# Head results of a two-layer hybrid encoder: adding two partial products ahead of the transposes, two heads to a set of four

## The chip, the cores and the metric

The kernel runs on one core of one Trainium2 chip. The metric is the device time of one execution in microseconds (us). The core has a matrix engine (PE, with its weight loads shown as PEld), a vector engine (DVE), a scalar engine (ACT), GpSimd (POOL), and a queue (SP) that issues transfers.

## The reference

A trunk of two layers over 512 positions of width 1024. Each layer is a half-step SwiGLU block, a token mixing, and another half-step SwiGLU block; each is normalised, shifted, scaled and gated by a conditioning vector. The change lies in the token mixing alone:

```python
oa, _ = banded_attention(qa, ka, va, A_HALF_WINDOW, sink)      # 8 query heads, 2 key heads
for window, dilation in B_BRANCHES:                            # 8 heads, three branches
    o, l = dilated_branch(qb, kb, vb, window, dilation)
...
ya = rmsnorm(oa.reshape(b, s, A_WIDTH), onorm_a)
yb = rmsnorm(ob.reshape(b, s, B_WIDTH), onorm_b)
return jnp.concatenate([ya, yb], axis=-1) @ w_out
```

Every head has dimension 64. Of the 16 heads of a layer, the eight "b" heads attend to all 512 keys under a mask and the eight "a" heads to a window of 128 on either side. Everything is float32.

## The kernel before

Products keep float32 accuracy by splitting an operand into a high and a low part (names ending in `h`/`hi` and `l`/`lo`) and adding several products. In the mixing, a layer's 16 heads run one after the other, the eight b heads (0 to 7) first and the eight a heads (8 to 15) next. Two consecutive heads, with `a` = 0 and 1, share one projected query tile.

A head's work (`class Head`) has four steps. `scores(qt)`, for each of four blocks of 128 queries, makes two score products (L655, L656), adds the mask and takes the row extreme on DVE (L660), and takes the exponential on ACT with the row sum into a column of `den` (L664). `exps` adds the sink term for a heads (L671, L672) and inverts `den` (L673). `pv(kt)`, for each of four blocks of keys, transposes the exponentials on PE (L685), splits them on ACT and DVE (L688, L689), and accumulates two products into the PSUM tile `po` (L692, L693). The stationary operand there is `V2[kt][:, vh]`, whose 128 columns are the 64 of the high part of the values and the 64 of the low part. So `po` is 128 partitions by 512 queries: partitions 0 to 63 hold the result of the high part and 64 to 127 that of the low part. `finish` copies `po` to SBUF as `oT` (L697, ACT), transposes it in four blocks of 128 queries (L700, PE, into the PSUM tile that the code calls `p2` and the trace `p`), copies the 64 columns of the low part into the output `o` or `oa` (L702, ACT), adds the 64 columns of the high part (L703, DVE), and multiplies by the inverted sums (L704, DVE).

The tile `oT` has the tag `acc` with one buffer, which the accumulator of the next norm uses as well. The PSUM tiles `po` and `p2` come out of the pool `pm` with the tag `mm`, four banks that the projections and the output products also use.

The order on the engines is settled when the program is built: a planner with costs of its own takes the instructions by priority as their inputs come due, and each engine then runs its list in order. `heads_` gives the order in which the steps are written: while head n does `pv`, head n+1 does `scores`, then `finish` of head n follows.

```python
for j in range(4):
    cur.pv(j)
    ...
    if nxt:
        nxt.scores(j)
...
with tc.high_priority(offset=HF if (n, 4) in after else 0):
    cur.finish()
```

`weave` puts fill work between these steps: the projections of queries, keys and values (L215 to L217, L624 to L626) beside the b heads, and the half of the output product that needs the b heads alone (`fill_a`) from head 10 on. After head 7 `branch_norm(o)` normalises the b results (L767 to L777); `branch_t` transposes them (L783) at four places of heads 9 and 10. After head 15 the same happens to the a results, and `out_tiles` makes the other half of the output product. The weight splits (L146, L147), the residual (L366), the rotary embedding (L575 to L581) and the split of the values (L633, L634) share ACT, DVE and POOL with the heads.

Of the kernel before, what the change touches and what calls it, by code (L numbers as in the profile page):

```python
# [10 lines left out]
F32 = mybir.dt.float32  # L11
F32R = mybir.dt.float32r
I32 = mybir.dt.int32
AF = mybir.ActivationFunctionType
ALU = mybir.AluOpType
# [4 lines left out]
S = 512  # L20
# [39 lines left out]
def tile_trunk(ctx: ExitStack, tc: tile.TileContext, xT, c, positions, adaT, cols, sink, wi1, wo1,  # L60
               wqk, wv, w_out, wi2, wo2, masks, freqs, out):
    nc = tc.nc
    V, A, T, G = nc.vector, nc.scalar, nc.tensor, nc.gpsimd
# [4 lines left out]
    nrm = ctx.enter_context(tc.tile_pool(name="nrm", bufs=2))  # L68
    tiny = ctx.enter_context(tc.tile_pool(name="tiny", bufs=4))
# [492 lines left out]
    def mixer(l, norm, pool, mod):  # L562
# [47 lines left out]
        def vproj():  # L610
            for _ in range(4):
                V2.append(pool.tile([128, 10, 2, 64], F32R, tag=f"v{len(V2)}", name="v2"))
            for a in range(2):
# [21 lines left out]
                                        op=ALU.subtract)  # L635
                vdone.append(a)

        class Head:
            def __init__(self, q, a, k, ka, vh, o, oc, windowed, sc):
                self.q, self.a, self.k, self.ka, self.vh = q, a, k, ka, vh  # L640
                self.o, self.oc, self.sc = o, oc, sc
                self.win = windowed
                self.rng = [(max(qt - 1, 0), min(qt + 2, 4)) if windowed else (0, 4) for qt in range(4)]
                self.sm = []

            def scores(self, qt):
                if qt == 0:
                    self.nb = tiny.tile([128, 4], F32, tag="nb", name="nb")
                    self.den = tiny.tile([128, 4], F32, tag="den", name="den")
                k0, k1 = self.rng[qt]  # L650
                w = (k1 - k0) * 128
                ks = slice(k0 * 128, k1 * 128)
                p = pq.tile([128, S], F32, tag="s", name="s")
                lq = self.q[:, self.a, qt * 128:qt * 128 + 128]
                T.matmul(p[:, :w], lq, self.k[0][:, self.ka, ks], start=True, stop=False)  # L655
                T.matmul(p[:, :w], lq, self.k[1][:, self.ka, ks], start=False, stop=True)  # L656
                s = pool.tile([128, S], F32, tag="sm", name="sm", bufs=5)
                m0 = 896 + (128 if qt == 0 else 0) if self.win else 384 - 128 * qt
                least = 3.0e38 if self.sc is None else nsnk[:, self.sc:self.sc + 1]
                V.tensor_tensor_reduce(out=s[:, :w], in0=p[:, :w], in1=mask[:, m0:m0 + w], scale=-0.125,  # L660
                                       scalar=least, op0=ALU.add, op1=ALU.min,
                                       accum_out=self.nb[:, qt:qt + 1])
                self.sm.append(s)
                A.activation(s[:, :w], s[:, :w], AF.Exp, scale=-1.0, bias=self.nb[:, qt:qt + 1],  # L664
                             accum_out=self.den[:, qt:qt + 1])
# [27 lines left out]
                T.matmul(po, lv, pl[:, :w], start=False, stop=kt == 3, skip_group_check=self.win)  # L693

            def finish(self):
                oT = nrm.tile([128, S], F32, tag="acc", name="oT", bufs=1)
                A.activation(oT, self.po, AF.Copy)  # L697
                p2 = pm.tile([128, 4, 128], F32, tag="mm", name="p2")
                for qt in range(4):
                    T.transpose(p2[:, qt], oT[:, qt * 128:qt * 128 + 128], ident)  # L700
                od = self.o()[:, :, self.oc * 64:self.oc * 64 + 64]
                A.activation(od, p2[:, :, 64:128], AF.Copy)  # L702
                V.tensor_tensor(od, p2[:, :, 0:64], od, op=ALU.add)  # L703
                V.tensor_tensor(od, od, self.den[:, :, None].to_broadcast([128, 4, 64]), op=ALU.mult)  # L704

        def heads(makers, hp, after):
            it = heads_(makers, after)
# [295 lines left out]
    for l in range(L):  # L1003
        if l:
            with tc.tile_pool(name="ffn", **FP) as pool:
                ada["pool"] = pool, 1
                ada_list += [(1, ch, k) for ch in range(6, 9) for k in range(KD)]
                norm = ffn(l, 0, norm, pool, ada_step, mod=(fin[:, l, 4], fin[:, l, 3]))
                while ada_list:
                    ada_step()  # L1010
        with tc.tile_pool(name="mix", **FP) as pool:
            norm = mixer(l, norm, pool, (fin[:, l, 7], fin[:, l, 6]))
        with tc.tile_pool(name="ffn", **FP) as pool:
            ada["pool"] = pool, 1
            if l == 0:
                ada_list += [(1, ch, k) for ch in range(2, 6) for k in range(KD)]

            def gain(m, s):
                xg = pool.tile([128, 1024], F32, tag=f"s{'hl'[m % 2]}{m // 2}", name="xg")[:, :S] if s.start == 0 else xgs[m]
                if s.start == 0:  # L1020
                    xgs.append(xg)
                A.activation(xg[:, s], x[:, m, s], AF.Copy, scale=col[:, C_FIN + m:C_FIN + m + 1])

            xgs = []
            norm = ffn(l, 2, norm, pool, ada_step, None, gain if l == L - 1 else None,
                       (fin[:, 1, 1], fin[:, 1, 0]))
            while ada_list:
                ada_step()
            if l == L - 1:
                final_out(norm, xgs, pool)  # L1030
# [83 lines left out]
```

## Time and profile before

| | |
|---|---|
| median of 3 runs | 1953.99 us (1951.84 to 1955.06) |
| the profiled execution, its time | 1955.42 us |
| its span, first to last instruction | 1953.6 us |
| mean granted clock of PE, share of full speed | 0.993 |

The span is what the trace covers; 1.8 us of the profiled execution's time lie around it. An engine's busy time is the sum of its instructions' durations with overlaps taken once. Matrix products are pipelined, so the cost of one in a busy stretch is the distance from its start to the next one's start, not its duration.

### The profile page before, as it was taken

How to read it: one execution, taken by the hardware profiler on the slowest of the kernel's cores; microseconds unless marked ns; L12 is line 12 of the kernel's file. 1: busy time of each engine (PE TensorE's matmuls, PEld its weight loads, DVE VectorE, ACT ScalarE, POOL GpSimd, SP SyncE). 2: the span in 40 equal slices, each digit the busy share in tenths (PEclk: the TensorE clock that was granted, in tenths of full speed). 3: DMA queues.
4: the chain of work that ended last, by engine and by line, in shares of the span. 5: the costliest groups of instructions: out<-in, count | busy, mean ns of one | idle time of the engine just before them, and what ended most of it. 6: DMA issues, size and time to landing. Idle time of an engine off the chain costs nothing.

```text
span 1953.6 us, 31187 instructions
## 1 busy us (share of the span) xinstructions
PE 1915.1 (98%) x12064; PEld 1718.1 (88%) x12064; DVE 1510.1 (77%) x2713; ACT 939.2 (48%) x1798; POOL 94.9 (5%) x69
## 2 busy tenths in 40 slices
PE   7999999999999999999999999999999999999998
PEld 5788888898778999989999897999977899898998
DVE  7988833477798988889589797876778989686773
ACT  5422222246585644536445262553556856353552
POOL 4000000011210000000000000000212000000000
PEclk8999999999999999999999999999999999999999
DMA  7889833244422154553415554242534113233231
GB/s 257 294 303 324 315 108 97 74 124 119 132 60 69 65 193 164 185 181 124 136 55 165 171 167 156 87 141 79 151 108 119 44 44 104 102 106 120 85 112 44
DMA packets 85111, 267.98 MB, mean 137 GB/s; under 512 B 10721, under 2 KB 13921, under 8 KB 84962
## 3 DMA queue, kind: packets, MB, share of 16 engines
q1 hardware_dynamic: 84962, 265.98, 41.8%
q8 instruction: 95, 1.56, 0.3%
q14 instruction: 54, 0.44, 0.1%
HBM read 244.97 MB, written 2.10 MB: 126 GB/s over the span
## 4 chain that ended last, share of the span: by engine, by line
PE 77%; DMA 9%; DVE 8%; issue 3%; ACT 2%; SPq 1%; POOL 0%; DVEq 0%; ACTq 0%; POOLq 0%
PE mm L217 14%; PE mm L216 14%; PE mm L215 14%; PE mm L457 9%; PE mm L458 8%; PE mm L459 8%; DMA araw<-in_adaT_dram 8%; DVE araw L302 3%; PE ptr L685 2%; DVE lo L147 1%; PE po L692 1%; PE po L693 1%; PE s L655 1%; PE s L656 1%; PE mm L624 1%
## 5 line engine op out<-in xcount | busy, mean ns | idle before, releaser
L146 ACT ACTIVATE hi<-raw 128x1024 fp32r<-128x1024 f32 (+5 forms) x251 | 213.8, 867 | 293.8 <-PE mm L217 201.8
L147 DVE TENSOR_TENSOR lo<-raw,hi 128x1024 fp32r<-128x1024 f32 (+5 forms) x251 | 258.1, 1039 | 74.3 <-ACT hi L146 73.4
L215 PE MATMUL mm<-hh,hi 128*128 128x512 f32 (+1 forms) x864 | 307.2, 357 | 7.4 <-ACT hh L286 6.8
L217 PE MATMUL mm<-hl,hi 128*128 128x512 f32 (+1 forms) x864 | 304.4, 357 | 2.7 <-DVE hl L287 2.7
L216 PE MATMUL mm<-hh,lo 128*128 128x512 f32 (+1 forms) x864 | 306.3, 356 | 0.0
L215 PE MATMUL mm<-gh,hi 128*128 128x512 f32 (+1 forms) x832 | 298.2, 358 | 5.5 <-ACT gh L507 5.5
L217 PE MATMUL mm<-gl,hi 128*128 128x512 f32 (+1 forms) x832 | 298.5, 359 | 0.5 <-DVE gl L441 0.2
L216 PE MATMUL mm<-gh,lo 128*128 128x512 f32 (+1 forms) x832 | 298.2, 358 | 0.0
L457 PE MATMUL mm<-sh,hi 128*128 128x256 f32 x912 | 260.4, 286 | 3.3 <-ACT sc L479 2.6
L458 PE MATMUL mm<-sh,lo 128*128 128x256 f32 x912 | 258.0, 283 | 0.0
L459 PE MATMUL mm<-sl,hi 128*128 128x256 f32 x912 | 257.9, 283 | 0.0
L302 DVE CUSTOM_DVE_ANT_0 araw<-araw,cs 128x1024 f32<-128x1024 f32 x136 | 167.7, 1236 | 57.9 <-DMA araw<-in_adaT_dram 57.5
L174 ACT ACTIVATE hi<-raw 128x512 fp32r<-128x512 f32 x228 | 132.9, 623 | 142.9 <-issue 74.3
L215 PEld LDWEIGHTS mm<-hh,hi 128*128 128x128 f32 x864 | 164.6, 191 | 29.9 <-ACT hh L286 8.1
L366 DVE SCALAR_TENSOR_TENSOR x<-mm,fin,x 128x512 f32<-128x512 f32 (+1 forms) x156 | 101.8, 653 | 114.3 <-PE mm L217 113.8
L217 PEld LDWEIGHTS mm<-hl,hi 128*128 128x128 f32 x864 | 164.1, 191 | 25.7 <-DVE hl L287 4.0
L215 PEld LDWEIGHTS mm<-gh,hi 128*128 128x128 f32 x832 | 157.8, 190 | 29.5 <-ACT gh L507 6.8
L216 PEld LDWEIGHTS mm<-hh,lo 128*128 128x128 f32 x864 | 164.5, 191 | 21.2
L217 PEld LDWEIGHTS mm<-gl,hi 128*128 128x128 f32 x832 | 158.1, 190 | 25.3 <-DVE gl L510 1.8
L457 PEld LDWEIGHTS mm<-sh,hi 128*128 128x128 f32 x912 | 174.1, 191 | 4.6 <-ACT sc L479 3.0
L216 PEld LDWEIGHTS mm<-gh,lo 128*128 128x128 f32 x832 | 158.1, 190 | 22.1
L458 PEld LDWEIGHTS mm<-sh,lo 128*128 128x128 f32 x912 | 174.3, 191 | 0.0
(188 smaller groups left out, 4043.7 us busy)
## 6 DMA issues: line engine op xcount, KB each, us to landing
raw<-in_wi_dram SPq DMA_DIRECT2D x170, 512.0 KB, 3.3
araw<-in_adaT_dram SPq DMA_DIRECT2D x144, 512.0 KB, 4.6
raw<-in_wo_dram SPq DMA_DIRECT2D x64, 448.0 KB, 4.1
raw<-in_wo_dram SPq DMA_DIRECT2D x32, 512.0 KB, 3.6
raw<-in_wqk_dram SPq DMA_DIRECT2D x26, 512.0 KB, 3.4
raw<-in_w_out_dram SPq DMA_DIRECT2D x16, 512.0 KB, 3.3
kh<-qh SPq DMA_DIRECT2D x40, 128.0 KB, 2.4
kl<-t SPq DMA_DIRECT2D x40, 128.0 KB, 2.3
```

What stands on the lines that cost most here:

```text
L146: A.activation(hi[:, sl], raw[:, sl], AF.Copy)
L147: V.tensor_tensor(lo[:, sl], raw[:, sl], hi.bitcast(F32)[:, sl], op=ALU.subtract)
L174: A.activation(d, r, AF.Copy)
L215: T.matmul(ps, wh, X[0][:, s], start=start, stop=False)
L216: T.matmul(ps, wl, X[0][:, s], start=False, stop=False)
L217: T.matmul(ps, wh, X[1][:, s], start=False, stop=stop)
L302: return V.tensor_tensor_reduce(out=raw, in0=raw, in1=cs, scale=1.0, scalar=0.0, op0=ALU.mult, op1=ALU.add, accum_out=mod[:, l, ch, k:k + ...
L366: V.scalar_tensor_tensor(x[:, m, s], ps[:, s], gate[:, m:m + 1], x[:, m, s], op0=ALU.mult, op1=ALU.add)
L457: T.matmul(ps, wh, xh, start=start and k == 0, stop=False, skip_group_check=True)
L458: T.matmul(ps, wl, xh, start=False, stop=False, skip_group_check=True)
L459: T.matmul(ps, wh, xl, start=False, stop=stop and k == 3, skip_group_check=True)
L685: T.transpose(p[:, j * 128:j * 128 + 128], self.sm[qt][:, c0:c0 + 128], ident)
```

## The change

Two heads share one tile `den` (`two`, one column for each) and one tile `oT`. Each head copies the 64 partitions of the other part of its `po` to its own half of `oT` (partitions 0 to 63 for `a` = 0, 64 to 127 for `a` = 1) on ACT, and adds the 64 partitions of its own part on DVE. Only the second head of two then makes the four transposes, and one DVE multiplication over 512 columns writes the results of both heads, straight out of PSUM. The copy L702 and the two DVE steps over 256 columns (L703, L704) are gone.

```diff
+        two, halves = [], []
+
         class Head:
             def __init__(self, q, a, k, ka, vh, o, oc, windowed, sc):
+                if a == 0:
+                    two.append(tiny.tile([128, 4, 2], F32, tag="den", name="den"))
+                self.two = two[-1]
+                self.den = self.two[:, :, a]
...
-                    self.den = tiny.tile([128, 4], F32, tag="den", name="den")
...
             def finish(self):
-                oT = nrm.tile([128, S], F32, tag="acc", name="oT", bufs=1)
-                A.activation(oT, self.po, AF.Copy)
+                if self.a == 0:
+                    halves.append(nrm.tile([128, S], F32, tag="acc", name="oT", bufs=1))
+                oT = halves[-1]
+                own, other = (slice(64 * j, 64 * j + 64) for j in (self.a, 1 - self.a))
+                A.activation(oT[own], self.po[other], AF.Copy)
+                V.tensor_tensor(oT[own], self.po[own], oT[own], op=ALU.add)
+                if self.a == 0:
+                    return
                 p2 = pm.tile([128, 4, 128], F32, tag="mm", name="p2")
                 for qt in range(4):
                     T.transpose(p2[:, qt], oT[:, qt * 128:qt * 128 + 128], ident)
-                od = self.o()[:, :, self.oc * 64:self.oc * 64 + 64]
-                A.activation(od, p2[:, :, 64:128], AF.Copy)
-                V.tensor_tensor(od, p2[:, :, 0:64], od, op=ALU.add)
-                V.tensor_tensor(od, od, self.den[:, :, None].to_broadcast([128, 4, 64]), op=ALU.mult)
+                c0 = self.oc * 64 - 64
+                od = self.o()[:, :, c0:c0 + 128].rearrange("p q (a d) -> p q a d", d=64)
+                V.tensor_tensor(od, p2.rearrange("p q (a d) -> p q a d", d=64),
+                                self.two[:, :, :, None].to_broadcast([128, 4, 2, 64]), op=ALU.mult)
```

## Rows read from the trace of the kernel before

**Rows 1.** The profile's page: span, engines (busy us, share, instructions), granted clock in 40 slices.

```profile
span 1953.6 us, 31187 instructions
...
PE 1915.1 (98%) x12064; PEld 1718.1 (88%) x12064; DVE 1510.1 (77%) x2713; ACT 939.2 (48%) x1798; POOL 94.9 (5%) x69
...
PEclk8999999999999999999999999999999999999999
```

**Rows 2.** The page's chain that ended last, shares of the span by engine.

```profile
PE 77%; DMA 9%; DVE 8%; issue 3%; ACT 2%; SPq 1%; POOL 0%; DVEq 0%; ACTq 0%; POOLq 0%
```

**Rows 3.** Busy time by stretch: b heads, a heads (layer 1, layer 2), after them.

```profile
core 0: us, PE busy (x) PEld busy (x) DVE busy (x) ACT busy (x) POOL busy (x), PEclk, DMA share, GB/s
430.00:558.00 128.00, 125.73 (x675) 102.57 (x673) 97.69 (x205) 79.57 (x168) 25.37 (x19) 1.00 0.43 117
558.00:617.00 59.00, 58.06 (x342) 48.20 (x342) 54.87 (x166) 45.30 (x126) 2.60 (x2) 1.00 0.17 50
1372.00:1498.00 126.00, 124.30 (x687) 103.86 (x686) 91.92 (x182) 71.96 (x144) 27.77 (x20) 1.00 0.48 134
1498.00:1560.00 62.00, 60.53 (x365) 49.88 (x364) 58.02 (x173) 50.34 (x143) 6.43 (x5) 1.00 0.19 52
1560.00:1580.00 20.00, 19.87 (x113) 16.95 (x112) 16.52 (x38) 9.61 (x19) 0.00 (x0) 1.00 0.29 95
```

**Rows 4.** Groups of finish by shape: busy us, mean ns, idle before and releaser.

```profile
L700 PE MATMUL p<-ident,oT 128*128 128x128 f32 x128 | 23.1, 279 | 0.2
...
L697 ACT ACTIVATE oT<-po 128x512 f32<-128x512 f32 x32 | 19.1, 595 | 22.1 <-PE po L693 22.0
...
L704 DVE TENSOR_TENSOR oa<-oa,den 128x256 f32<-128x256 f32 x16 | 7.8, 491 | 0.0
...
L703 DVE TENSOR_TENSOR o<-p,o 128x256 f32<-128x256 f32 x16 | 6.7, 416 | 0.9 <-ACT o L702 0.8
L704 DVE TENSOR_TENSOR o<-o,den 128x256 f32<-128x256 f32 x16 | 6.7, 416 | 0.1
L703 DVE TENSOR_TENSOR oa<-p,oa 128x256 f32<-128x256 f32 x16 | 6.6, 416 | 0.1
...
L702 ACT ACTIVATE oa<-p 128x256 f32<-128x256 f32 x16 | 6.1, 380 | 1.2 <-PE p L700 1.2
L702 ACT ACTIVATE o<-p 128x256 f32<-128x256 f32 x16 | 6.0, 377 | 0.5 <-PE p L700 0.5
```

**Rows 5.** The groups by shape: a DVE sum of PSUM and SBUF, 512 columns.

```profile
L496 DVE TENSOR_TENSOR sg<-mm,sc 128x512 f32<-128x512 f32 x57 | 39.0, 683 | 1.9 <-PE mm L459 1.9
```

**Rows 6.** The chain in order of time: start, us on the chain, what.

```profile
1481.29 0.44 PE p L700 x4
...
1556.92 0.44 PE p L700 x4
```

**Rows 7.** Timeline, DVE: two instructions back to back (start, us).

```profile
1510.40 0.42 DVE L689 TENSOR_TENSOR pl<-ptr,ph 128x256 fp32r<-128x256 f32 x1
1510.74 0.68 DVE L769 CUSTOM_DVE_ANT_0 sqo<-o 128x512 f32<-128x512 f32 x1
```

**Rows 8.** Timeline, ACT and PE: two copies to oT and the transposes after them.

```profile
448.82 0.60 ACT L697 ACTIVATE oT<-po 128x512 f32<-128x512 f32 x1 [0.79 <-PE po L693]
...
462.06 0.63 PE L700 MATMUL p<-ident,oT 128*128 128x128 f32 x4
...
1519.90 0.58 ACT L697 ACTIVATE oT<-po 128x512 f32<-128x512 f32 x1
...
1520.54 0.66 PE L700 MATMUL p<-ident,oT 128*128 128x128 f32 x4
```

**Rows 9.** Tile oT: idle time of PE until ACT wrote it (us, times).

```profile
  ACT oT L697: 3.9, 14
```

## Prediction

> **What bounds the kernel now.** I read the page first, for the engine without room. PE is busy for 1915.1 of 1953.6 us, DVE for 77% and ACT for 48%, and the clock is full but for the first slice [rows 1]. Busy PE time is modelled, so I turned to the chain that ended last: PE holds 77% of it and DVE 8% [rows 2]. Work taken off PE should therefore shorten the run, unless the stage in which it lies is held by something else. That needs the view by stretch. The change acts in two places of each layer. In the stretches of the b heads PE is busy 125.73 of 128 and 124.30 of 126 us, DVE only 97.69 and 91.92: PE binds. In those of the a heads PE is busy 58.06 of 59 and 60.53 of 62, but DVE 54.87 and 58.02, or 93% and 94% [rows 3]. There the two are nearly level, and which one gives way decides what the change is worth.
>
> Last I read the parts of `finish` themselves: the groups by shape for durations, the chain for what transposes really cost, and the timeline for how closely PE follows ACT.
>
> **PE, what is removed.** Now 32 heads make four transposes each, 128 in all; afterwards 16 pairs make four each, 64. The group's 279 ns is the duration of one [rows 4], but they overlap: on the chain four take 0.44 us together [rows 6], 0.11 each. Removing 64 saves 64 x 0.11 = 7.0 us of PE, 3.5 in the b stretches and 3.5 in the a stretches.
>
> **ACT.** Two copies of `po` remain for each pair. They now cover 64 partitions by 512 columns; no row has 64 partitions. If time goes by columns, each stays at 0.595 us [rows 4]; if by area, it falls toward the 0.377 of 256 columns [rows 4]. I take 0.595, because in the same group of instructions 128 partitions cost no more than the columns need. The 32 copies L702 go, 6.1 + 6.0 = 12.1 us of ACT [rows 4]. ACT does not bind, so I count this at nothing on the path; its cover is PE in the b stretches and DVE in the a stretches, and without a cover it would be a gain.
>
> **DVE.** Removed are four instructions of 256 columns for each pair, in all 6.7 + 6.6 + 6.7 + 7.8 = 27.8 us [rows 4]. Added are two sums of 64 x 512 and one product of 128 x 512. The nearest row is a sum of PSUM and SBUF over 512 columns at 0.683 us [rows 5]; 48 of these make 32.8 us. DVE so gains 5.0 us of work, 2.5 of it with the a heads, 1.25 in each layer. From below, if a sum over half the partitions cost as little as 256 columns (0.416), the new work is 16 x (0.416 + 0.416 + 0.683) = 24.2 us, a saving of 3.6. From above, if no new instruction overlapped its neighbours and the product cost two of 256 columns: now a DVE instruction of 0.42 us is followed after 0.34 [rows 7], an overlap of 0.08, so 16 x (2 x 0.763 + 0.832) = 37.7, or 9.9 more. I keep 5.0, because lanes standing idle do not shorten a stream of 512 columns on the other 64.
>
> The same overlap bears on one rule. The Trainium skill, in "VectorE: DVE Perf Modes", section "Two Vector instructions with no wait between them", says that an instruction whose input starts in another group of 32 partitions than the last one's is held until all earlier ones have finished. By that rule the sum of every second head, which starts at partition 64, and the instruction behind it would lose the overlap: an estimate of 16 x 2 x 0.08 = 2.6 us more of DVE, a total of 7.6 in place of 5.0; no row of before has such a start, so the trace neither bears it out nor speaks against it.
>
> **The wait ahead of the transposes.** Now PE waits for ACT alone: 14 times, 3.9 us in all [rows 9]. Afterwards it waits for ACT and then DVE, with half as many occasions. In the b stretches the transposes can stand far behind the copy (448.82 and 462.06), in the a stretches they come 0.64 us after its start, as soon as the copy ends [rows 8]. Behind a waiting transpose in PE's list stand the transposes and scores of the next head, for which ACT and DVE wait in turn. The added time in the pair's chain is one sum, 0.68 us, and what stands ahead of it on DVE. Fewer occasions against longer ones: I leave the 3.9 us as they are; the bounds are all of them gone, and the exposed case among the rivals.
>
> **Edits at nothing.** `den` in two columns changes no count; should the second head's first exponential wait for the first head's inversion, that inversion is earlier in the written order, and otherwise it costs ACT some tenths of a us in a stretch with room [rows 3]. `po` is held for one sum longer, about 0.7 us, while `p2` takes a PSUM bank half as often; I set these against each other, covered by the other banks. `oT` is held over two heads, but its next writer comes a head later. Behind heads 7 and 15 the chain to `branch_norm` loses the L702 copy and one 256-column step and gets two steps of 512 for two of 256, about 0.2 us; after head 15 the output product keeps PE busy 19.87 of 20 us [rows 3], which hides that.
>
> **The sum.** The b stretches, bound by PE, give all of their 3.5 us. In the a stretches PE falls by 3.5 us and DVE rises by 2.5 in the two layers, with DVE the fuller list afterwards. Between giving 3.5 and losing 2.5 I take half of the PE saving, 1.75, since DVE still has 4 us idle in each of these stretches [rows 3]. Together 5.25. The profiled execution of 1955.42 (span 1953.6, and 1.8 around it) becomes 1950.2; it stood 1.4 above the median of 1953.99, which becomes 1948.7.
>
> **Rivals.**
>
> *Full gain.* PE binds throughout, and halving the occasions takes most of the oT waits too: 7.0 to 7.0 + 3.9 = 10.9 us, 1943.1 to 1947.0. For it: PE is over 97% busy even with the a heads [rows 3]. Against: DVE at 93% there gets more work.
>
> *DVE takes it back.* In the a stretches DVE binds: its 2.5 us (by the bound above, 5.0) come onto the path and the 3.5 of PE there are worth nothing. With the 3.5 of the b stretches that is -1.0 to +1.5, or 1953 to 1955.5. For it: DVE's 54.87 of 59 [rows 3]. Against: DVE's lists there still show 4 us idle.
>
> *Slower: transposes exposed.* PE reaches the transposes right after the copy, as at 1520.54, and stands for the sum and the instruction ahead of it on DVE, 0.68 + about 0.6 = 1.28 us a pair. If the eight pairs of a heads pay, that is 10.2 - 7.0 = +3.2; if all sixteen, 20.5 - 7.0 = +13.5, 1967.5. It cancels the gain at 0.44 us a pair over sixteen, and makes the kernel slower by over 0.2% from 0.68. For it: the a heads' spacing [rows 8]. Against: the planner can put other products there, as it did at 448.82.
>
> **How the numbers follow.** No change, for a measurement of this kernel, is within 0.2%, 3.9 us: 1950.1 to 1957.9. The forecast has 0.40, with its own range 1946.5 to 1951.5, of which 0.33 lie below 1950.1. Full gain has 0.17; DVE takes it back 0.21, 0.18 of it within the bound and 0.03 above; exposed transposes 0.22, 0.04 of it within the bound (the a heads alone, 1957.2) and 0.18 above. That makes faster 0.33 + 0.17 = 0.50, same 0.07 + 0.18 + 0.04 = 0.29, slower 0.03 + 0.18 = 0.21. The range reaches from the full gain's lower end, 1943, into the exposed case, 1959, leaving out about 0.02 below and 0.16 above.
>
> **What would show it.** Right: 64 transposes of `oT` at 0.11 us on the chain; no copy L702; DVE sums near 0.68 us; the b stretches shorter by about 1.7 us in each layer and the a stretches by under 1. Wrong: sums at 0.42 or over 0.76 us; PE waiting for DVE's sum in `oT` for over 7 us in all; a stretches longer than 59 and 62 us with DVE at 97% or more; or a b stretch that does not shrink although PE lost its transposes, which would mean that another wait sets its end.

## The result, and the profile after

The changed kernel is slower: median 1966.16 us (1963.41 to 1968.06, 6 runs) against 1952.91 us for the kernel before in the same comparison, a ratio of 1.0071 with a 95% interval of 1.0058 to 1.0084. That is 13 us longer by the medians (14 by the ratio) where 5 us shorter was forecast, and outside the range. The profiled execution took 1968.06 us, its span is 1966.3.

The page of the changed kernel: span, engines, chain by engine, and q8, the queue that brings PE's instructions (packets, MB, share).

```profile
span 1966.3 us, 31039 instructions
...
PE 1914.2 (97%) x12000; PEld 1717.6 (87%) x12000; DVE 1520.9 (77%) x2697; ACT 935.0 (48%) x1766; POOL 97.9 (5%) x69
...
q8 instruction: 94, 1.54, 0.3%
...
PE 80%; DMA 8%; DVE 6%; issue 3%; ACT 2%; POOL 0%; SPq 0%; DVEq 0%; ACTq 0%; POOLq 0%
```

PE lost its 64 transposes and is busy 0.9 us less than in [rows 1]; DVE gained 10.8 us. To find the place, both traces were cut at the same events: a layer's first split of exponentials for head 0 and for head 8 (the ACT copies to `ph`), and one of the last updates of the residual in the mixing (of those over 256 columns the third in layer 1, the fifth in layer 2; what follows it in the mixing is as long as before). "b" is head 0 to head 8, "a" is head 8 to that update.

Busy time by stretch, changed kernel: b and a of layer 1, b and a of layer 2.

```profile
core 0: us, PE busy (x) PEld busy (x) DVE busy (x) ACT busy (x) POOL busy (x), PEclk, DMA share, GB/s
443.00:548.62 105.62, 104.22 (x545) 84.40 (x544) 83.54 (x161) 63.46 (x126) 22.56 (x17) 1.00 0.47 129
548.62:630.51 81.89, 75.26 (x428) 62.67 (x427) 72.43 (x195) 55.05 (x143) 4.65 (x3) 0.96 0.18 51
1405.55:1511.15 105.60, 104.21 (x545) 84.41 (x544) 83.48 (x161) 63.43 (x126) 22.56 (x17) 1.00 0.47 128
1511.15:1595.93 84.78, 78.16 (x452) 65.68 (x452) 74.63 (x199) 55.95 (x145) 4.65 (x3) 0.96 0.19 56
```

The same stretches of the kernel before.

```profile
441.07:550.15 109.08, 106.82 (x562) 86.39 (x561) 82.92 (x165) 64.90 (x133) 21.57 (x17) 1.00 0.46 128
550.15:625.68 75.53, 74.59 (x443) 62.23 (x442) 68.78 (x199) 55.91 (x152) 3.90 (x3) 1.00 0.19 56
1395.56:1504.63 109.07, 106.80 (x562) 86.38 (x561) 82.95 (x165) 64.92 (x134) 21.60 (x17) 1.00 0.46 128
1504.63:1583.02 78.39, 77.48 (x467) 65.09 (x466) 70.46 (x203) 56.73 (x154) 3.88 (x3) 1.00 0.18 56
```

Each b stretch is 3.46 us shorter, twice the forecast; each a stretch is 6.4 us longer. Ahead of head 0, where the order is unchanged, 1.2 and 1.0 us are lost, for a reason that no run shows. Taken together, layer 1 loses 4.1 us and layer 2 3.9. A further 4.2 us are lost between the two mixings, where no instruction and no order changed.

The groups of `finish` in the changed kernel (L707 is the copy, L708 the sum, L713 the transposes, L716 the product).

```profile
L708 DVE TENSOR_TENSOR oT<-po,oT 64x512 f32<-64x512 f32 x32 | 22.0, 686 | 9.9 <-ACT oT L707 9.7
L707 ACT ACTIVATE oT<-po 64x512 f32<-64x512 f32 x32 | 19.0, 594 | 22.2 <-PE po L698 21.6
L713 PE MATMUL p<-ident,oT 128*128 128x128 f32 x64 | 11.2, 288 | 0.0
...
L716 DVE TENSOR_TENSOR o<-p,den 128x512 f32<-128x512 f32 x8 | 5.5, 688 | 0.4 <-PE p L713 0.4
L716 DVE TENSOR_TENSOR oa<-p,den 128x512 f32<-128x512 f32 x8 | 5.4, 679 | 0.0
```

The sizes are as forecast from [rows 4, 5]: columns set the time, not partitions. PE waits for the sum 1.5 us in all, 6 times, less than for the copy in [rows 9]; so the transposes of `oT` are not what is exposed. What is new is one wait: in the a stretch of layer 2 PE's waits begin as follows (total, times, longest).

```profile
PE pty L796 <- DVE o L790: 5.0, 1, 5.0
PE mm L215 <- ACT yah L799: 0.9, 1, 0.9
```

These are the transposes of the normalised b results (`branch_t`, L783 before). Layer 1 has the wait too, 5.0 us. In the kernel before it is 0.2 us in layer 2.

```profile
PE pty L783 <- DVE o L777: 0.2, 1, 0.2
```

The timeline of DVE in the changed kernel shows what PE waits for: the chain from head 7's product (L716) over the squares (L782), the reciprocal root (L226 to L232) to the scaling (L790).

```profile
1515.10 0.69 DVE L716 TENSOR_TENSOR o<-p,den 128x512 f32<-128x512 f32 x1
...
1519.44 0.16 DVE L227 TENSOR_SCALAR r<-r 128x4 int32<-128x4 int32 x1
...
1520.31 0.15 DVE L229 TENSOR_TENSOR r<-r 128x4 f32<-128x4 f32 x1
1520.45 0.68 DVE L708 TENSOR_TENSOR oT<-po,oT 64x512 f32<-64x512 f32 x1
1521.06 0.14 DVE L230 TENSOR_TENSOR r<-r,r 128x4 f32<-128x4 f32 x1
...
1524.40 0.14 DVE L231 SCALAR_TENSOR_TENSOR r<-r 128x4 f32<-128x4 f32 x1
1524.46 0.68 DVE L147 TENSOR_TENSOR lo<-raw,hi 128x512 fp32r<-128x512 f32 x1
1525.06 1.22 DVE L232 SCALAR_TENSOR_TENSOR y<-r,r 128x4 f32<-128x4 f32 x1
1526.21 0.68 DVE L147 TENSOR_TENSOR lo<-raw,hi 128x512 fp32r<-128x512 f32 x1
1526.81 2.27 DVE L790 TENSOR_SCALAR o<-o,y 128x512 f32<-128x512 f32 x3
```

The first and the last step of the same chain in the kernel before, and its second L232.

```profile
1508.73 0.42 DVE L704 TENSOR_TENSOR o<-o,den 128x256 f32<-128x256 f32 x1
...
1516.32 0.15 DVE L232 SCALAR_TENSOR_TENSOR y<-r,r 128x4 f32<-128x4 f32 x1
...
1516.73 1.27 DVE L777 TENSOR_SCALAR o<-o,y 128x512 f32<-128x512 f32 x3
```

From the product's start to the end of the scaling are 14.0 us, where the kernel before needed 1508.73 to 1518.00, 9.3 us. Of the 4.7 us more, 2.1 are L232 and L790, which took longer beside a product on POOL (below); the others are instructions that now stand between the small steps of the chain, such as rotary steps and two weight splits. DVE has next to no idle time there, as the stretch from head 8's first split to the end of the scaling shows, first in the kernel before, then in the changed one.

```profile
1504.63:1518.00 13.37, 13.11 (x77) 10.32 (x75) 12.43 (x49) 12.06 (x35) 1.29 (x1) 1.00 0.18 45
```

```profile
1511.15:1529.10 17.95, 12.92 (x75) 10.85 (x75) 17.37 (x53) 12.45 (x35) 3.37 (x2) 0.94 0.13 40
```

The stall has a tail: PE was idle from 1523.44 to 1528.43, and in 1528.4 to 1536.0 its mean granted clock is 0.64 of the higher level (2.4 GHz), so part of it at the lower one (1.2 GHz); the a stretches show 0.96 where they showed 1.00.

```profile
1528.40:1536.00 7.60, 7.46 (x36) 6.63 (x36) 6.04 (x17) 4.50 (x12) 0.00 (x0) 0.64 0.37 104
```

Head by head, by the first split of each, the a stretch of the changed kernel is 1.3 us behind the kernel before at head 9, 6.0 at head 10 and 6.4 at its end: the loss falls in head 9, where this wait lies.

### The profile page after: what moved, and what is told of

Its sections match the earlier page's. It is cut to its first block, busy times and chain, and to the rows that moved or that the text cites. A ratio compares the mean times of both kernels' runs of the same rounds, so it can differ in the third digit from the quotient of the medians.

```text
span 1966.3 us, 31039 instructions
## 1 busy us (share of the span) xinstructions
PE 1914.2 (97%) x12000; PEld 1717.6 (87%) x12000; DVE 1520.9 (77%) x2697; ACT 935.0 (48%) x1766; POOL 97.9 (5%) x69
## 4 chain that ended last, share of the span: by engine, by line
PE 80%; DMA 8%; DVE 6%; issue 3%; ACT 2%; POOL 0%; SPq 0%; DVEq 0%; ACTq 0%; POOLq 0%
PE mm L217 15%; PE mm L215 15%; PE mm L216 15%; PE mm L457 8%; PE mm L458 8%; PE mm L459 8%; DMA araw<-in_adaT_dram 6%; PE ptr L690 2%; DVE araw L302 2%; PE po L697 1%; PE po L698 1%; PE s L660 1%; PE s L661 1%; DMA raw<-in_wi_dram 1%; PE mm L626 1%
## 5 line engine op out<-in xcount | busy, mean ns | idle before, releaser
L147 DVE TENSOR_TENSOR lo<-raw,hi 128x1024 fp32r<-128x1024 f32 (+5 forms) x251 | 257.5, 1036 | 75.6 <-ACT hi L146 74.6
```

The costliest lines, as they stand in the source:

```text
L147: V.tensor_tensor(lo[:, sl], raw[:, sl], hi.bitcast(F32)[:, sl], op=ALU.subtract)
```

## The experiments

All ratios are against the kernel before, with 95% intervals. The three columns behind them are the lengths of the stretches minus those of the kernel before, from the traces, in us; "between" is from the end of the first mixing to the start of the second; the last column is the median time from issue to landing of the 170 up-projection weights and the packets on queue q8.

| kernel | ratio | b, layer 1 / 2 | a, layer 1 / 2 | between | landing, q8 |
|---|---|---|---|---|---|
| the change | 1.0071 (1.0058 to 1.0084) | -3.5 / -3.5 | +6.4 / +6.4 | +4.2 | 3.7, 94 |
| before_again | 1.0005 (0.9995 to 1.0015) | -0.1 / 0.0 | 0.0 / 0.0 | -2.9 | 3.3, 95 |
| b_only | 1.0047 (1.0034 to 1.0061) | -3.5 / -3.5 | +5.2 / +6.5 | +3.8 | 3.7, 94 |
| a_only | 1.0065 (1.0043 to 1.0088) | 0.0 / +0.1 | +4.7 / +3.6 | +3.3 | 3.7, 94 |
| late | 1.0046 (1.0030 to 1.0062) | -3.5 / -3.5 | +6.0 / +5.9 | +2.3 | 3.7, 94 |
| nopool | 1.0087 (1.0063 to 1.0111) | -3.0 / -3.1 | +9.6 / +8.5 | +5.7 | 3.8, 94 |
| deferadd | 1.0078 (1.0059 to 1.0097) | -0.9 / -0.9 | +5.7 / +6.0 | +2.0 | 3.7, 94 |
| pe_sum | 1.0052 (1.0035 to 1.0068) | +0.4 / +0.4 | +3.0 / +3.0 | -4.1 | 3.3, 96 |
| dvework | 1.0038 (1.0026 to 1.0050) | 0.0 / +0.4 | +2.7 / +2.6 | -1.1 | 3.3, 95 |
| trim | 1.0024 (1.0013 to 1.0036) | -0.1 / 0.0 | -0.1 / 0.0 | +5.7 | 3.7, 94 |
| pad | 1.0134 (1.0112 to 1.0155) | -3.5 / -3.5 | +6.1 / +6.6 | -2.5 | 3.3, 95 |
| pad_tiny | 1.0071 (1.0050 to 1.0093) | -2.5 / -1.9 | +6.1 / +6.0 | -0.2 | 3.3, 95 |
| before_late | 1.0015 (1.0003 to 1.0027) | 0.0 / +0.1 | +1.5 / +1.7 | -0.4 | 3.3, 95 |
| b_late_pad | 1.0121 (1.0099 to 1.0142) | -3.5 / -3.5 | +5.3 / +5.1 | -4.8 | 3.3, 95 |
| b6_pad | 1.0029 (1.0018 to 1.0041) | -2.9 / -2.9 | +4.5 / +5.7 | +1.0 | 3.3, 95 |
| norm_act | 1.0019 (1.0008 to 1.0030) | -2.9 / -2.8 | +5.2 / +3.1 | -0.6 | 3.3, 95 |
| b_normact | 1.0000 (0.9990 to 1.0009) | -3.5 / -3.5 | +2.6 / +2.6 | -0.8 | 3.3, 95 |
| before_normact | 1.0057 (1.0041 to 1.0073) | 0.0 / +0.1 | +4.6 / +4.9 | -2.4 | 3.3, 95 |

The second row sets the scale. It is the kernel before with one priority changed to no effect on any engine's order: the stretches of the mixing repeat to 0.1 us, the part between the mixings only to some 3 us. In b6_pad, b_normact, before_normact and before_late the time lies outside what the theory and its rival gave; in pad and b_late_pad too, where the longer warm-up cost some 21 us at the start.

### Which heads lose, and where

**b_only and a_only** share the transposes for one kind of head; the other kind runs the old `finish`.

```diff
+                self.share = not windowed
...
             def finish(self):
+                if not self.share:
...
+                    return
```

(`windowed` in place of `not windowed` for a_only.)

> The change in the b heads alone; the a heads finish as in the kernel before. Theory 1 (the list of DVE between head 7's result and the scaled o has become longer: rotary steps and weight splits stand in it): those steps still stand there, only one sum of an a head is gone, so PE still idles 3 to 5 us before the transposes of o in each layer and the ratio is 1.002 to 1.006. Theory 2 (the a heads' sums on DVE cost the time): the loss is gone and 32 transposes are saved, ratio 0.997 to 0.999.

> The change in the a heads alone; heads 0 to 7 finish as in the kernel before. Theory 1: head 7's result comes as before, and of the steps between it and the scaled o only one sum of 0.69 us and other fill are new, so PE idles 0 to 3 us before the transposes of o in each layer, ratio 0.997 to 1.002. Theory 2 (the a heads' sums on DVE cost the time): nearly the whole loss stays, ratio 1.004 to 1.008.

The gain of the b stretch belongs to the b heads alone and is the same in both kernels that have it, 3.5 us. The loss does not. b_only came out as its theory 1 has it, a_only in time as theory 2: b_only, whose a heads are untouched, loses 5.2 and 6.5 us in the a stretches, and a_only 4.7 and 3.6. They don't add up to the 6.4 of both together. PE's wait for the scaled `o` is 4.4 us a layer in b_only and 2.1 in a_only, 5.0 with both.

**late** moves the transposes of the normalised b results one head back, **before_late** does so in the kernel before.

```diff
-HJ = [(9, 2), (9, 3), (10, 0), (10, 1)]
-HN = 10
+HJ = [(10, 0), (10, 1), (10, 2), (10, 3)]
+HN = 11
```

> The changed kernel with the four transposes of the normalised b results moved later: places (10,0) to (10,3) in place of (9,2) to (10,1), and the first half of the output product from head 11 instead of 10. Theory 1 (PE reaches these transposes before DVE has scaled o: 5.0 us of idle PE in each layer and some 1.7 us behind it at half clock, 13 us in all): the idle time of PE until DVE wrote o falls from 10.0 us to under 2, no half clock in the mixing, and the time falls by 9 to 14 us, to 0.996 to 1.001 of the kernel before. Theory 2 (the sums over 64 partitions fill DVE, and the a heads' stretches are held by it): the waits move elsewhere, the ratio stays at 1.005 to 1.008.

> The kernel before with nothing but the later transposes of the normalised b results (all four in head 10). In the kernel before PE doesn't wait for them, so nothing is to be gained there: 1953 to 1957. If the earlier place costs something unseen in the kernel before too, it is 2 to 4 us faster, and a gain of the run with shared b heads would be that of the place and not of the change.

In late the stall is gone and the clock stays at 1.00, yet the a stretch is only 0.4 us shorter than in the change: PE now waits for its scores (1.3 us for `nb` in layer 1), for the results' split (0.8) and for `oT` (0.7). By the first split of each head it is only 0.5 us behind the kernel before at head 12, and 6.1 at head 14. So the loss in head 9 goes with the wait, and a new one of about its size comes behind head 12; why there, no run shows. The later place alone costs 1.5 and 1.7 us a layer.

**nopool** puts the rotary products of the last two projections (L577, L581), which ran on POOL beside the long L232 and L790 above, on DVE.

```diff
-        def rope(p, kind):
+        def rope(p, kind, G=G):
...
-                yield from proj(kind, st)
+                yield from proj(kind, st, V if n >= 7 else G)
```

> The changed kernel with the two POOL products of the rotary embedding (L577, L581) on DVE for the last two query projections of each layer. In the changed kernel two steps of the chain to o took about 1 us longer each while POOL worked beside them (1.22 us for 128x4, 2.27 for three of 0.48). If POOL's work is what makes the chain late, the chain loses 2.1 us and PE's idle time before the transposes of o falls from 5.0 to about 3 us in each layer, ratio 1.003 to 1.006. If it is only the order on DVE, the idle time stays at 5 us or grows by the 0.7 us steps that come to DVE, ratio 1.007 to 1.010.

L232 is 0.16 us again and the three scalings take 1.27 in place of 2.27, so the stretching came with POOL's work. The wait fell from 10.0 to 4.3 us in all, but the a stretches grew by another 2 to 3 us. The products now stand on DVE; that they are what costs this is likely, but not shown apart from the new order.

### Whose time runs out

**deferadd** writes the sum, and what follows it, one step later.

```diff
-                V.tensor_tensor(oT[own], self.po[own], oT[own], op=ALU.add)
+                self.rest = oT, own
+
+            def finish2(self):
+                oT, own = self.rest
+                V.tensor_tensor(oT[own], self.po[own], oT[own], op=ALU.add)
```

> The changed kernel with the sum, the transposes and the product of each head (heads 7 and 15 excepted) written one step later, behind the next head's first pv, so that ACT's copy of po has ended when DVE comes to the sum. If DVE's standing for that copy (9.7 us in 14 waits in the changed kernel) is what holds the steps behind it and PE in turn, those waits fall under 3 us and the ratio falls to 0.998 to 1.003. If the work on DVE is what costs, the waits go and the ratio stays at 1.005 to 1.008.

The b stretch keeps 0.9 us of its gain and the a stretch is still 5.7 and 6.0 us longer. DVE's waits for the copy fell only to 6.8 us (10 times), not under 3, so this run doesn't tell whether they matter.

**pe_sum** is the kernel before, with the two parts added by PE: in place of the transposes a product of `oT` with two stacked identities, 64 columns wide. The copy L702 and the sum L703 are gone.

```diff
-                    T.transpose(p2[:, qt], oT[:, qt * 128:qt * 128 + 128], ident)
+                    T.matmul(p2[:, qt], oT[:, qt * 128:qt * 128 + 128], dup, start=True, stop=True)
```

> From the kernel before: each head keeps its copy to oT, but the four transposes become products with two identities of 64 stacked to 128 x 64, so that PE adds the two parts as it transposes; ACT's copy L702 and DVE's sum L703 are gone for all 32 heads (12.1 us of ACT, 13.3 of DVE), PE keeps 128 such products. If DVE's work and its waits in the a heads' stretches are what binds there, this gains 3 to 8 us (0.996 to 0.9985) although PE makes no fewer products; if PE alone binds, the ratio is 0.999 to 1.002, or more where a product of 64 columns costs PE more than the 0.11 us of a transpose.

**dvework** is the kernel before with one more instruction of 256 columns on DVE for each pair of a heads, 1.65 us a layer, into a scratch tile.

```diff
+                if self.win and self.a:
+                    V.tensor_tensor(more, more, p2[:, :, 0:64], op=ALU.min)
```

> From the kernel before: DVE makes one instruction of 256 columns more for each two a heads, behind the product of the second one, on data that nothing else uses; it waits for nothing new and nothing waits for it. That is 1.65 us more of DVE in each layer, more than the 1.25 that the change adds there. If work on DVE binds in the a heads' stretches, the ratio is 1.0015 to 1.003 (3.3 us and more in all); if the changed kernel's loss is in its waits and its order, the ratio is 0.999 to 1.001.

In dvework the a stretches are 2.7 and 2.6 us longer for 1.65 us of work each, and the run 5 to 10 us longer for 3.3. The order changed with the work, though: the third update of the residual in layer 1's a stretch comes 40.9 us into it, where it came after 47.0. pe_sum takes 12.7 us off DVE and 8.4 off ACT in the run (1497.4 and 930.8 busy) and gives PE 8.5 more; its a stretches are 3.0 us longer, and PE is busy 78.14 of 78.49 us in layer 1's. So the a stretch has little room on either engine: work added to DVE lengthens it, and so does work added to PE.

**b6_pad** shares the transposes for the b heads 0 to 5 alone, so that head 7's `finish` and all a heads are those of the kernel before.

```diff
+                self.share = not windowed and oc < 6
```

> Shared transposes for b heads 0 to 5 alone; heads 6 and 7, behind which the b results are normalised, and all a heads as in the kernel before. The warm-up is one-column products and two of 512 columns, so that PE's list is as long as before. Theory (the b heads give 3.46 us a layer, a quarter of it with heads 6 and 7; the loss lies behind head 7 and in the a heads' DVE work): 2.6 us a layer, 5.2 in all, 0.9973, with raw<-in_wi at 3.3 us. Rival (whatever the b heads gain is given back with the a heads, because DVE's work there sets the end): 0 to 2 us, 0.999 to 1.0.

The b stretch gains 2.9 us, and PE then waits 2.9 us for the scaled `o`. This is DVE in the kernel b6_pad:

```profile
1509.44 0.42 DVE L714 TENSOR_TENSOR o<-o,den 128x256 f32<-128x256 f32 x1
...
1513.49 0.69 DVE L578 TENSOR_TENSOR t<-t,part 128x512 f32<-128x512 f32 x1
...
1516.22 0.93 DVE L229 TENSOR_TENSOR r<-r 128x4 f32<-128x4 f32 x1
...
1517.78 0.72 DVE L575 STREAM_SHUFFLE part<-mm 128x512 f32<-128x512 f32 x1
...
1518.81 1.22 DVE L232 SCALAR_TENSOR_TENSOR y<-r,r 128x4 f32<-128x4 f32 x1
1519.95 0.68 DVE L147 TENSOR_TENSOR lo<-raw,hi 128x512 fp32r<-128x512 f32 x1
1520.55 1.27 DVE L805 TENSOR_SCALAR o<-o,y 128x512 f32<-128x512 f32 x3
```

From head 7's product to the end of the scaling: 12.4 us, with the same steps of the chain as in the kernel before, where it was 9.3. What lies between them is different: a rotary step (L578) that came ahead of the product before, and another (L575) and a split (L147) that came behind the scaling. And L229 and L232 took 0.93 and 1.22 us in place of 0.15 beside POOL's products, 1.9 us of the 3.1. The shorter b stretch took nothing off DVE (83.54 us busy in layer 1's, 82.92 before); PE arrives early and waits.

### Giving DVE room

**norm_act** is the change, with PE's list padded (below), and in the norms of the head results all four squares and three of the four scalings on ACT; **b_normact** the same with shared transposes for the b heads alone; **before_normact** the same moves in the kernel before.

```diff
-                if qt % 2:
+                if True:
...
-                if qt == 3:
+                if qt >= 1:
```

> As pad_tiny, and in both norms of the head results all squares and three of the four scalings run on ACT in place of DVE, some 2.5 us of DVE less behind head 7 and as much behind head 15 in each layer. Theory (behind head 7 and with the a heads DVE's list sets the end, at about two us for one as the added work showed): the stall ahead of the transposes of the b results falls from 5 us to under 2.5 in each layer and the run is 5 to 10 us shorter than pad_tiny, 0.998 to 1.0015. Rival (ACT or the chain itself sets the end, not DVE's list): the stall stays, within 2 us of pad_tiny.

> Shared transposes for the b heads alone, PE's list padded, and the norms of the head results with all squares and three of four scalings on ACT, as in norm_act. Theory (the b heads gain 3.46 us a layer on PE and lose it, because behind head 7 DVE's list is full; with 2.5 us less on DVE there the stall shrinks to under 2 us): a mixing 1 to 3 us shorter than in the kernel before, 0.9965 to 0.999. Rival (the end of the a heads gives it back anyway): 1.0005 to 1.003.

> The kernel before with only the squares and scalings moved to ACT. It tells what of b_normact and norm_act is the moved work alone. Theory (DVE sets the end with the a heads in the kernel before too, at two us for one as the added work showed): 2 to 4 us a layer, 0.996 to 0.998, so that it beats every version with the change. Rival (in the kernel before DVE's 4 idle us are enough and PE sets the end): within 1 us, 0.9995 to 1.0005.

norm_act is 9 us faster than the same kernel without the moves (pad_tiny: medians 1956.15 and 1965.03), and the wait for `o` fell from 10.0 to 4.6 us. In b_normact it is 1.4 us, the a stretches lose only 2.6 us, the mixings, with what lies ahead of head 0, are 0.8 us shorter and 0.5 longer than before, and the run is level with the kernel before. In the kernel before, the same moves cost 10 us. There PE's waits have a new row (total, times, longest):

```profile
PE ptr L685 <- ACT sm L664: 4.7, 2, 2.4
```

That is 2.4 us a layer, about half of the loss there, and its place is the order on ACT behind head 7. ACT in before_normact:

```profile
555.28 0.63 ACT L767 ACTIVATE sqo<-o 128x512 f32<-128x512 f32 x1
...
557.12 0.62 ACT L767 ACTIVATE sqo<-o 128x512 f32<-128x512 f32 x1
...
557.73 0.29 ACT L671 ACTIVATE es<-nb,snk 128x4 f32<-128x4 f32 x1
...
558.40 0.51 ACT L664 ACTIVATE sm<-sm,nb 128x256 f32<-128x256 f32 x1
```

ACT in b_normact:

```profile
548.62 0.62 ACT L673 ACTIVATE sm<-sm,nb 128x384 f32<-128x384 f32 x1 [0.24 <-DVE nb L669]
...
549.24 0.28 ACT L680 ACTIVATE es<-nb,snk 128x4 f32<-128x4 f32 x1
...
549.80 0.62 ACT L795 ACTIVATE sqo<-o 128x512 f32<-128x512 f32 x1
```

In the one the sink term and the exponentials of the next head come behind the four squares, in the other ahead of them. ACT is about equally busy in layer 1's a stretch, 60.6 and 59.9 us. So moving work off DVE isn't worth a fixed amount; it depends on where the planner puts it. Every run here kept the priorities and fill rates of the kernel before (HP, HB, HA, FB and FA), and only late, before_late and b_late_pad moved HJ and HN. Whether other settings would let the changed kernel keep its gain was not tried.

**b_late_pad** combined the b heads' sharing, the later place of late and a padded list.

> The shared transposes for the b heads alone, the normalised b results transposed one head later (all four places in head 10), and the padded warm-up. If the three costs are apart and add up (a heads' own share, the 4.4 us stall ahead of the b results' transposes in each layer, the transfers), none is left: b_only's 1.0047 gives back 9 us of stall and 5 of transfers, 1947 to 1952. Rival, the stall only moves to a wait of the same size in heads 9 and 10, as it did with both kinds of heads changed: 1955 to 1960.

The stall is gone and the a stretches are 5.3 and 5.1 us longer all the same (start: +22 us by the padding).

### The transfers between the mixings

In every kernel of the change that left PE's list shorter, the weights landed in 3.7 or 3.8 us, in every other in 3.3. Three kernels tell the length of the list from the rest. **trim** is the kernel before with its warm-up products replaced by two of 512 columns; **pad** is the changed kernel with the warm-up cut into quarters; **pad_tiny** the changed kernel with one-column products in the warm-up. **before_again** is the control.

```diff
-WARM = (8, 6, 4)
+WARM = (1, 1, 0)
...
-            T.matmul(p[:, :128], ident, ident, start=True, stop=True)
+            T.matmul(p.rearrange("p (a b) -> p a b", a=4), ident, ident[:, None, :].to_broadcast([128, 4, 128]),
+                     start=True, stop=True)
```

The inner lines of `warm` in pad and in pad_tiny (the latter with 49 products and WARM = (1, 0, 0)):

```diff
+        for j in range(4 * n):
+            T.matmul(p[:, :32], ident, ident[:, j % 4 * 32:j % 4 * 32 + 32], start=True, stop=True)
...
+        for j in range(49):
+            T.matmul(p[0:1, 0:1], ident[:, 0:1], ident[:, 0:1], start=True, stop=True)
```

And before_again:

```diff
-HF = 300
+HF = 301
```

> The kernel before once more, with the same instructions in the same order on every engine, to see how far its profile repeats. In the profile of the changed kernel and of four variants the weights of the gated blocks took 3.7 us to land against 3.3 in the kernel before, and the block between the two mixings was 2 to 6 us longer although its order is the same. If that belongs to the chip and the moment and not to the change, this profile shows 3.7 us and a block as long as in the variants, or lies between, with a time within 0.2% of the kernel before. If it belongs to the change, it shows 3.3 us and the old block.

> The kernel before with the 18 warm-up products replaced by two of 512 columns, which makes PE's list about as much shorter as the change did. Theory, length of the list: q8 shows 94 packets, raw<-in_wi lands in 3.7 us, and the run is 3 to 7 us longer than the kernel before. Rival, the transfers are the change's own: 95 packets or 94, but 3.3 us, and 0 to 1 us (a few tenths for a colder start).

> The changed kernel with the 18 warm-up products ahead of the first block cut into 72 of a quarter of the columns, so that PE's list of instructions is again at least as long as in the kernel before. Theory, the slower weight transfers follow the length of PE's list (94 packets of instructions on queue q8 in every kernel with 3.7 us, 95 or 96 in every one with 3.3): q8 shows 95 or 96, raw<-in_wi lands in a median of 3.3 us, and the run loses about 5 of the change's 13 us, 1958 to 1962. Rival, the transfers are slower for what the change itself does (the place of den, the order of the heads): 3.7 us and 1965 to 1969 as before.

> The changed kernel with the same cheap padding of PE's list, so that it is as long as before. Theory (the list's length makes the weight transfers slower, which cost the kernel before 5.7 us between its two mixings): raw<-in_wi lands in 3.3 us, q8 shows 95 packets, and 5 to 7 us of the change's 13 come back, ratio 1.003 to 1.0045. Rival (the transfers cost the changed kernel nothing beyond what the mixings lose): 1.0065 to 1.0075.

The DMA views of trim, first the queue of PE's instructions (95 packets in the kernel before), then the weights (3.3 us there).

```profile
q8 instruction: 94, 1.54, 0.3%
...
raw<-in_wi_dram SPq DMA_DIRECT2D x170, 512.0 KB, 3.7
```

In trim nothing in the mixings moved, the weights land 0.4 us later, and all of the loss, 5.7 us, lies between the mixings; the run is slower by 2.4 thousandths (2.5 to 7.0 us). Both paddings bring the landing back to 3.3 us. Over all kernels of the table the part between the mixings is +2.0 to +5.7 us with 94 packets (seven kernels) and -4.8 to +1.0 with 95 or 96 (eleven). So the landing time follows the list's length: trim shortens it, the paddings lengthen it, and the landing goes along both ways. What it is worth in the changed kernel's time is less sure: pad_tiny's span is 3.5 us shorter than the change's, but its timed ratio, 1.0050 to 1.0093, is no better and excludes the 1.0030 to 1.0045 expected of it. And pad pays 21 us at the start, for its 144 short warm-up passes took 31 us of PE.

## Why the prediction was wrong

**What bounds the kernel.** Reading the b stretches as PE's and the a stretches as nearly level was right. The conclusion for the a stretches, a term of the sum, was not: "nearly level" was taken as "half of the saving is kept", 1.75 us in both layers, "since DVE still has 4 us idle". They lost 12.8. Little of those 4 us lies where it was needed: behind head 7, DVE had 0.9 of 13.37 us idle. The sign "DVE at 97% or more" did not come for the whole stretch either (72.43 of 81.89 us), only behind head 7 (17.37 of 17.95). Of the seventeen experiments, the two that left the mixing's order alone repeat the a stretch to 0.1 us, and each of the others has it longer, by 1.5 to 9.6 us, whichever engine it relieves.

**PE.** Four transposes take 0.44 us on the chain as before (0.71 behind the stall), and the b stretches give 3.46 us each, not 1.75. This term was too small: of the 3.46, 2.6 are PE's busy time (106.82 to 104.22) and 0.9 its waits (2.26 to 1.40). That busy time fell by more than 16 transposes at 0.11 was only seen, not traced further.

**DVE.** The durations held (0.686, 0.688 and 0.679 us), and so did the price of the change's own instructions: their durations add 2.5 us a layer, as forecast. The total did not: DVE's busy time over both stretches rises by 4.3 us in layer 1 (151.70 to 155.97). Most of the rest is the 2.1 us of L232 and L790 beside POOL; lost overlap adds some 0.7, and other steps took about 1 us less. The Trainium skill, in "VectorE: DVE Perf Modes", section "Two Vector instructions with no wait between them", has an instruction held whose input starts in another group of 32 partitions than the last one's. The trace agrees: the sum at partition 0 that started at 1520.45 was followed after 0.61 us, the one at partition 64 below after 0.73. Of the 16 sums at partition 64 none overlapped the instruction before or behind it; of the 16 at partition 0, 12 were overlapped by the next one.

```profile
1513.43 0.69 DVE L708 TENSOR_TENSOR oT<-po,oT 64x512 f32<-64x512 f32 x1
1514.16 0.62 DVE L665 CUSTOM_DVE_ANT_0 sm<-s,mask,nsnk 128x384 f32<-128x384 f32 x1
```

**The wait ahead of the transposes** was put at 3.9 us and became 1.5. The rival "transposes exposed" thus had the right side for a reason that did not occur. Instead DVE waits 9.7 us, 14 times, for ACT's copies, nearly all in the b stretches, where it has room.

**Edits at nothing** is the step that failed. It took the chain from head 7 to `branch_norm` as "about 0.2 us" longer and named a cover only for head 15, the output product. Behind head 7 no cover was named, and there was none: the chain became 4.7 us longer, and PE stood 5.0 us in each layer and ran part of the 7.6 us behind that at the lower clock. What the runs showed in its place is that DVE's list is full there. The shorter b stretch takes nothing off it, so the 3.46 us that PE wins beside the b heads end in front of it: b6_pad, with the chain's steps and all a heads as before, has PE wait 2.9 us, b_only 4.4. norm_act, which takes steps off DVE there, halves the wait and is 9 us faster than pad_tiny. How the order on DVE came to hold more ahead of the scaling is the planner's doing and was not traced. Nor is the wait the whole account, since late removes it and loses as much behind head 12. The rival "DVE takes it back" named this mechanism, but priced it with the change's own 2.5 to 5 us in both layers, from the a heads. It missed that DVE also holds what PE wins in the stretch ahead.

**ACT at nothing.** No run speaks against it: ACT is busy 55.05 of 81.89 us in the a stretch, and no wait of PE or its weight loads for ACT grew there by more than 1.2 us (for `sm`, 0.4 to 1.6).

**The transfers.** No step allowed for them; a shorter list of PE instructions was counted as a pure gain. In the profile the part between the mixings is 4.2 of the 12.7 us by which the span grew, though that part repeats only to some 3 us, and pad_tiny, with the landing back at 3.3 us, was no faster by its time.

## What to carry to other kernels

Where two engines are both above 90% busy, as in these a stretches, taking work from one may only move the wait; carry the saving forward to the next place where the other engine must have delivered, and price it there. Read how many us of idle time it has at that place, not over the whole stretch. For every chain of small dependent steps, ask what the scheduler can put between them once its inputs come earlier. In such a stretch the same move can have either sign: squares and scalings on ACT were worth 9 us with the change and cost 10 without it, so each needs its own run.

## What the runs showed of the hardware that was not expected

The landing time of weights on their queue follows the number of PE instructions in the program: 94 packets of instructions on queue q8 go with 3.7 or 3.8 us, 95 or 96 with 3.3, also where the kernel is otherwise the same (trim). Why is open.

While POOL worked on a product of 128 by 512, a DVE step on 128 by 4 took 1.22 us in place of 0.15, and three scalings 2.27 in place of 1.27; with POOL's work moved away they were short again. POOL in the changed kernel:

```profile
1524.64 1.62 POOL L577 TENSOR_TENSOR part<-part,rs 128x512 f32<-128x512 f32 x1 [14.25 <-DVE r L231]
1526.23 1.78 POOL L581 TENSOR_TENSOR t<-t,qh 128x512 f32<-128x512 f32 x1
```

L232, started during the first product, ended with it (1526.28 and 1526.26). In b6_pad L229 and L232 ended within 0.03 us of a product on POOL too. Not every step is held: the splits L147 that had started just ahead of each of these products kept their 0.68 us, and the products took 1.62 and 1.78 us where most take 1.29.

A product with 128 by 32 moving columns in the warm-up takes 0.215 us a pass (112 in 24.10, run pad), one of one row and column 0.027 (58 in 1.59, run b6_pad).
